# A convolution's last load in odd-sized pieces: 5, 120 and 3 partitions for the last quarter

## The chip, the cores and the metric

One core of a Trainium2 chip. The metric is the device time of one execution in microseconds (us). A ratio below is the mean time of one kernel's fast runs over that of the other's of the same rounds, so it is not quite the ratio of the medians that are quoted; an interval is a 95% interval. A few executions of 130.3 to 130.5 us are slow and count nowhere.

## The reference

```python
# x: (16, 64, 64, 64) float32, weight: (128, 64, 3, 3) float32, 90% zeros
x_pad = np.pad(x, ((0, 0), (0, 0), (1, 1), (1, 1)))
for b, co, ci, kh, kw in ...:      # five nested loops
    output[b, co] += weight[co, ci, kh, kw] * x_pad[b, ci, kh:kh+64, kw:kw+64]
# output: (16, 128, 64, 64) float32, 33.55 MB
```

## The kernel before

The 16 images go in 8 pairs; a pair fills 128 partitions (2 images of 64 channels). GpSimd issues the loads, which cast float32 to bf16 on the way (all but the weights and the first half of pair 0, which SyncE loads as they are); SyncE issues the stores. TensorE forms the products, GpSimd one sum of two rows per block, ScalarE and VectorE bring the results to the output tiles.

```python
xs = [x_pool.tile([128, H, W], BF16, name=f"x{p}") for p in range(NP)]   # all 8 pairs stay in SBUF
...
nc.gpsimd.dma_start(out=xs[0][:, HEAD:H, :], in_=pair(0)[:, HEAD:H, :])  # software queue
...
for p in range(1, NP):
    nc.gpsimd.dma_start(out=xs[p], in_=pair(p))       # 128 rows of 16 KB float32 -> 8 KB bf16
... # warm-up matmuls, weights
for p in range(NP):
    o = [o_pool.tile([C_OUT, H, W], FP32, name="o") for _ in range(2)]
    for blk in range(4):
        ... # GpSimd: s = even rows + odd rows of xs[p]; TensorE, ScalarE, VectorE: o
        if last and blk % 2 == 1:
            ... # store half of each o: 128 rows of 8 KB (4 stores in all)
    if not last:
        for n in range(2):
            nc.sync.dma_start(out=out[2 * p + n], in_=o[n])   # 128 rows of 16 KB (14 stores)
```

## Time and profile before

| | before |
|---|---|
| time, median | 127.65 us (3 runs), 127.64 (6 runs) |
| profiled execution | 127.12 us, span 125.4 us |
| last TensorE instruction | 110 us |
| last store issued / last landing | 111.8 / 124.2 us |
| bytes stored, share of the DMA engines' time | 66.2% of 16 engines' span, the loads 30.7% |

The page's rows of digits are tenths of busy time in 40 slices of the span. The lines that matter stand in the prediction. Beside them I used the trace's records of single DMA packets (queue, start, duration, size). A packet of an engine begins where the engine's last one ended, to a few ns, so in the last part of the run, with only stores left, the packets can be put together into 16 sequences, one for each DMA engine. Where loads and stores alternate this is ambiguous.

### The profile page before, as it was taken

The page shows a single profiled execution, that of the slowest core. Times are in us where ns is not written, and L with a number is a line of the kernel's source. Part 1 is how long each engine was busy: PE and PEld are TensorE (multiplying, and loading weights), DVE is VectorE, ACT ScalarE, POOL GpSimd, SP SyncE. Part 2 cuts the span into 40 slices and gives each one's busy share as a digit, 9 for nine tenths or more (in the row PEclk, how much of TensorE's full clock was granted, in tenths as well). Part 3 has the DMA queues.
Part 4 walks back from the last instruction along what each step waited for, and adds up shares of the span by engine and source line. Part 5 has one row for each costly group of instructions (what it writes and reads, how often), then busy time and mean ns, then how long its engine had stood idle before and what let it go on. Part 6 is the DMA issues. An engine that isn't in the chain of part 4 may idle for free.

```text
span 125.4 us, 2486 instructions
## 1 busy us (share of the span) xinstructions
PE 107.5 (86%) x1002; PEld 58.8 (47%) x1002; DVE 82.4 (66%) x135; ACT 39.0 (31%) x71; POOL 40.7 (32%) x45
## 2 busy tenths in 40 slices
PE   6679999999999999999999999999999999920000
PEld 6435555555555555555555555555555555500000
DVE  0463877877787778777877787778777877760000
ACT  4555323333333333333333333333333333300000
POOL 6936533333333333333333333333333300000000
PEclk9999999999999999999999999999999999997555
DMA  5999999989999999999999999999999999999980
GB/s 146 338 222 220 212 214 220 191 259 350 324 311 337 308 293 319 342 316 308 426 429 423 408 429 434 450 416 434 418 418 429 429 444 423 434 397 423 423 369 10
DMA packets 4044, 42.93 MB, mean 342 GB/s; under 512 B 448, under 2 KB 448, under 8 KB 704
## 3 DMA queue, kind: packets, MB, share of 16 engines
q1 hardware_dynamic: 2880, 34.90, 66.2%
q0 software_dynamic: 1152, 7.86, 30.7%
q8 instruction: 8, 0.13, 0.4%
q14 instruction: 4, 0.03, 0.1%
HBM read 17.07 MB, written 33.55 MB: 404 GB/s over the span
## 4 chain that ended last, share of the span: by engine, by line
PE 81%; DMA 4%; DVE 1%; issue 1%; DVEq 0%; SPq 0%
PE ps L135 81%; DMA o<-in_x_dram 4%; DVE o L168 1%; DVEq L214 0%; DVE x L87 0%; SPq L60 0%; DVEq L168 0%
## 5 line engine op out<-in xcount | busy, mean ns | idle before, releaser
L168 DVE TENSOR_TENSOR o<-ps,pc 128x512 f32<-128x512 f32 x124 | 77.8, 686 | 22.1 <-PE ps L135 19.8
L135 PE MATMUL ps<-x,wT 64*128 64x504 bf16 (+3 forms) x780 | 88.8, 373 | 1.5 <-DVE x L87 1.5
L135 PEld LDWEIGHTS <-wT 64*128 64x128 bf16 x966 | 55.2, 94 | 49.4 <-issue 1.5
L154 POOL TENSOR_TENSOR s<-x 128x512 bf16<-128x512 bf16 x31 | 35.6, 1152 | 57.7 <-PE ps L135 41.5
L161 ACT COPY pc<-ps 128x512 f32<-128x512 f32 x62 | 33.3, 589 | 64.0 <-issue 61.8
L135 PE MATMUL ps<-s,wT 64*128 64x512 bf16 (+1 forms) x186 | 25.7, 377 | 0.0
L74 PE MATMUL ps<-idle_rhs 128*128 128x128 bf16 x27 | 3.1, 310 | 1.0 <-DVE idle_rhs L71 1.0
L67 POOL DMA_DIRECT2D x<-in_x_dram x7 | 3.7, 561 | 0.0
L74 PEld LDWEIGHTS <-idle_rhs 128*128 128x128 bf16 x27 | 2.8, 144 | 1.0 <-DVE idle_rhs L71 1.0
L91 DVE CAST w_bf<-w_sb 128x192 bf16<-128x192 f32 (+1 forms) x4 | 1.3, 382 | 3.0 <-DMA w_sb<-in_weight_dram 3.0
L149 DVE COPY o<-ps 128x512 f32<-128x512 f32 x2 | 1.4, 692 | 2.0 <-PE ps L135 2.0
L148 ACT COPY o<-ps 128x512 f32<-128x512 f32 x2 | 1.2, 586 | 2.4 <-PE ps L135 2.4
L87 ACT CAST x<-o 128x576 bf16<-128x576 f32 (+1 forms) x2 | 1.5, 802 | 0.5 <-DMA o<-in_x_dram 0.5
L91 ACT ACT_TABLE_LOAD x1 | 1.3, 1283 | 0.7 <-PEq L203 0.7
L97 PE MATMUL ps<-ident,w_bf 128*128 128x128 bf16 x9 | 1.1, 292 | 0.4 <-DVE w_bf L91 0.4
L87 DVE CAST x<-o 128x576 bf16<-128x576 f32 x1 | 0.5, 460 | 1.4 <-DMA o<-in_x_dram 1.4
L91 ACT CAST w_bf<-w_sb 128x64 bf16<-128x64 f32 (+1 forms) x2 | 0.7, 418 | 1.9 <-DMA w_sb<-in_weight_dram 1.9
L97 PEld LDWEIGHTS <-w_bf 128*128 128x128 bf16 x9 | 0.8, 128 | 0.8 <-DVE w_bf L91 0.8
L101 DVE TENSOR_TENSOR wT<-ps,wT 128x384 bf16<-128x384 f32 x2 | 1.0, 550 | 0.0
L63 POOL DMA_DIRECT2D x<-in_x_dram x1 | 0.7, 696 | 0.8 <-POOLq L203 0.8
L71 DVE MEMSET idle_rhs<- 128x64 uint32 x1 | 0.1, 112 | 0.8 <-PEq L203 0.8
L110 ACT CAST wT<-ps 128x384 bf16<-128x384 f32 x1 | 0.5, 481 | 0.4 <-PE ps L97 0.4
(8 smaller groups left out, 1.9 us busy)
## 6 DMA issues: line engine op xcount, KB each, us to landing
out_dram<-o SPq DMA_DIRECT2D x14, 2048.0 KB, 19.8
x<-in_x_dram POOLq DMA_DIRECT2D x7, 1024.0 KB, 29.3
out_dram<-o SPq DMA_DIRECT2D x4, 1024.0 KB, 12.3
o<-in_x_dram SPq DMA_DIRECT2D x1, 1024.0 KB, 5.4
x<-in_x_dram POOLq DMA_DIRECT2D x1, 512.0 KB, 7.5
w_sb<-in_weight_dram SPq DMA_DIRECT2D x1, 288.0 KB, 3.1
```

The lines of the kernel that those rows point to most:

```text
L67: nc.gpsimd.dma_start(out=xs[p], in_=pair(p))
L74: nc.tensor.matmul(idle_ps, idle_rhs, idle_rhs, start=True, stop=True)
L87: copy(out=xs[0][:, a:b, :], in_=x_head[:, a:b, :])
L91: copy(out=w_bf4[:, g, a:b, :], in_=w_v[:, k : k + b - a, :])
L97: nc.tensor.matmul(wps[:, j, :], src, ident, start=True, stop=True)
L101: nc.vector.tensor_tensor(out=wT[:, g], in0=wps, in1=wT[:, G1], op=SUB)
L135: nc.tensor.matmul(ps[n][:, lo:hi, c_lo:c_hi], tap(g, kw, n), src[q, a:b:step, c_lo + kw - 1 : c_hi + kw - 1], start=(i == 0), stop=(i == ...
L148: nc.scalar.copy(out=o[0][:, r0 : r0 + rows, :], in_=ps[0])
L149: nc.vector.tensor_copy(out=o[1][:, r0 : r0 + rows, :], in_=ps[1])
L154: nc.gpsimd.tensor_tensor(out=s, in0=xs[p][:, r0 : r0 + 16 : 2, :], in1=xs[p][:, r0 + 1 : r0 + 16 : 2, :], op=ADD)
L161: nc.scalar.copy(out=c, in_=shared[n])
L168: nc.vector.tensor_tensor(out=o[n][:, first : r0 + 16 : 2, :], in0=ps[n], in1=pc[n], op=ADD)
```

## The change

Its intent: one DMA engine (number 4) ends last, so the last load is cut and issued such that GpSimd's rotation over the engines gives that engine the least.

```diff
-    for p in range(1, NP):
+    for p in range(1, NP - 1):
         nc.gpsimd.dma_start(out=xs[p], in_=pair(p))
...
+    PIECES = (            # (issued at pair, first and last partition, first and last image row)
+        (2, 0, 128, 0, 48),
+        (3, 0, 5, 48, 64),
+        (3, 5, 125, 48, 64),
+        (4, 125, 128, 48, 52),
+        (4, 125, 128, 52, 56),
+        (4, 125, 128, 56, 60),
+        (4, 125, 128, 60, 64),
+    )
     for p in range(NP):
...
+        for when, c0, c1, a, b in PIECES:
+            if when == p:
+                nc.gpsimd.dma_start(
+                    out=xs[NP - 1][c0:c1, a:b, :], in_=pair(NP - 1)[c0:c1, a:b, :]
+                )
```

## The prediction

> **What bounds the kernel now.** I read, in this order, the page's utilisation rows, the chain of waits, SyncE's own waits, a table of windows, and last the single DMA packet records of the trace (queue, start, duration, size of each; they do not name the DMA engine). The page first:
>
> ```profile
> PE   6679999999999999999999999999999999920000
> DVE  0463877877787778777877787778777877760000
> DMA  5999999989999999999999999999999999999980
> ...
> q1 hardware_dynamic: 2880, 34.90, 66.2%
> q0 software_dynamic: 1152, 7.86, 30.7%
> ```
>
> TensorE and VectorE stop about 15 us before the end. The DMA row is 9 from slice 2 to slice 38: the 16 DMA engines never rest, and the two queues' shares, 66.2% and 30.7%, fill the span. What ends the program is the last store, not arithmetic:
>
> ```profile
> SPq L188 <- DVE o L168: 92.2, 14, 19.9
> SPq L214 <- DMA out_dram<-o: 11.6, 4, 4.4
> ```
>
> The second line is SyncE waiting 11.6 us for the last stores after it issued them. The windows table (span, then busy times; last three columns are granted clock, DMA share, GB/s) shows how that end looks:
>
> ```profile
> 64.00:110.00 46.00, 46.00 (x434) 24.58 (x431) 35.89 (x58) 15.17 (x29) 12.97 (x12) 1.00 1.00 427
> ...
> 121.50:122.50 1.00, 0.00 (x0) 0.00 (x0) 0.00 (x0) 0.00 (x0) 0.00 (x0) 0.50 0.43 180
> 122.50:123.70 1.20, 0.00 (x0) 0.00 (x0) 0.00 (x0) 0.00 (x0) 0.00 (x0) 0.50 0.06 27
> ```
>
> A DMA share of 1.00 through 46 us, and 0.06 in the last 1.2 us. One engine of sixteen is 0.0625, so **a single DMA engine works alone at the end**. The 16 completion events of each store say the same. Those of the last store land at 121.3, 121.3, 121.4, 121.6, 121.8, 122.2, 122.4, 122.5, four at 122.6, 122.7, 122.8, 122.8 and **124.2** us. The kernel is bound by the most loaded DMA engine, which is 1.4 us behind the second. The mean is 122.3, so perfect balance would be worth 124.2 - 122.3 = 1.9 us (1.5%).
>
> Why that engine is late is in the packets. From 62.5 us on, when only stores are left, one unbroken sequence of 16 KB store packets takes 634 to 662 ns each, where 1295 of the 1792 take 611 ns. It fills 62.5 to 110.2 us, some 74 rows at 646 ns against a period of 608 ns (from a store to the next the first engine takes 4.86 us for 8 rows): 74 x 38 ns = 2.8 us, and this engine ends 2.9 us after the first. The 8 instruction fetches (16 KB, 882 to 967 ns each) seem to fall on other engines, since the two packets after a fetch that take about 1 us are not in the slow sequence; they would account for the eight or so engines 1.1 to 1.5 us behind the first. That the slow engine is number 4 I take from the change; nothing in this trace numbers it.
>
> **What the Trainium skill says.** "DMA: Bandwidth & Descriptors", section "Why a DMA increments its semaphore by 16 and not by 1": a DMA is spread over the largest k up to 16 that divides its outer size; a software DMA with k below 16 takes k consecutive engines from a round-robin cursor, and all 16 engines post its completion increment. So 128 partitions use 16 engines, 5 use 5, 120 use 15, and 3 use 3. The trace agrees for 128 (1152 = 8 x (128 rows + 16 increments)) and has no other size. The same section names an exception: some software copies use ceil(partitions/16) per engine without the cursor; then the aim would miss. Section "Queues, rings and completion order": each engine takes turns between its queues, packet by packet. The trace agrees: between 22 and 62 us loads and stores alternate. Section "Latency and other measured facts" says engines 7 and 15 are usually slower in traces; here one is slow, and its cause is not shown.
>
> **The change, part by part.** The bytes loaded and stored are unchanged. Removed: one whole load of the last pair (128 rows of 16 KB float32, written as 8 KB bf16). Added: rows 0 to 47 of the image for 128 partitions (12 KB read per partition), then the last quarter (4 KB per partition) as 5 + 120 + 3 partitions, the 3 cut again into four of 1 KB.
>
> *Cursor.* If it stands at engine 0 (the 128-partition loads leave it), the 5 go to engines 0 to 4, the 120 to engines 5 to 15 and 0 to 3, so all but engine 4, eight each, and the four of 3 to engines 4 to 15, one each. Engine 4 gets one quarter row and one 1 KB piece; engines 0 to 3 nine quarter rows; the others eight and a 1 KB piece.
>
> *Cost of one packet.* A load packet of 16 KB read takes 624 ns and one of 8 KB 322 ns (the half load of pair 0). A line through both gives 20 ns + 37.75 ns per KB: 12 KB = 473, 4 KB = 171, 1 KB = 58 ns (estimates). Completion increments take 9 or 22 ns; six more DMAs put six more on each engine, about 0.09 us.
>
> *Sum per engine*, for the last pair's load:
> - before, every engine: 8 x 621 (start to start) = 4.97 us
> - after, engine 4: 8 x 473 + 171 + 58 + 90 = 4.10 us, **-0.87**
> - after, engines 0 to 3: 8 x 473 + 9 x 171 + 90 = 5.41 us, **+0.44**
> - after, engines 5 to 15: 8 x (473 + 171) + 58 + 90 = 5.30 us, **+0.33**
>
> All engines are busy without a break, so each engine's end moves by its sum: the slow one from 124.2 to 123.3, the second from 122.8 to between 123.1 and 123.25. They meet near 123.3: gain **0.9 us**, all on the path that sets the end.
>
> *GpSimd.* One load issue of 0.56 us leaves the start, seven come in later: one after the sum at 21.57 us (so near 22.7), two after that at 34.37 (35.5), four after that at 47.18 (48.3 to 50.5). GpSimd waits about 2.0 us before nearly every sum and is 2 blocks of 3.2 us ahead of TensorE, so even 4 x 0.56 = 2.2 us is absorbed. Two of the small pieces wait on a semaphore shared with earlier loads (pairs 4 and 5, landed at 33.4 and 43.2 us): past by then. No TensorE, VectorE or ScalarE instruction is added or removed; the order of some products in the last pair moves a little. Worth: 0.
>
> *Loads must not run dry.* The sixth pair's load lands at 53.0 us, and the pieces are in the ring by 50.5, so the two queues go on alternating. The load's last quarter now alternates 4 KB pieces with 16 KB stores and ends later than the 62.8 us of before: 53 + 8 x (0.47 + 0.61) + 8 x (0.17 + 0.61) is about 68 us. The last pair's first sum is at about 88.8 us and its rows 48 to 63 are wanted after 98: 20 us or more of slack.
>
> **Rivals.**
> - *The rotation misses the slow engine* (the cursor starts elsewhere, or the exception holds). Then it takes +0.33 to +0.44 like any other: 124.6, or 128.0 us on the clock. For it: nothing in the trace numbers engines or shows a cursor. Against: 5, 120, 4 x 3 fit the cursor rule so exactly that the slow engine was probably seen by number. I give it 15%.
> - *The second engine becomes the bound earlier*: if small packets cost more than the line says (a fixed 60 ns rather than 20 adds 8 x 40 = 0.3 us to all), the others end at 123.5: 127.0 us. For it: eight or nine engines lie within 0.4 us below the second. Against: the 4-byte increments cost only 9 to 22 ns.
> - *The late issue leaves the load queue empty or delays GpSimd.* The store queue would fill the engines anyway (a store takes 10.6 to 29.3 us to land, so stores are backed up), and total work decides: 0 to +0.3 us. The instants above speak against it.
> - *The slow engine's lag exists only under the profiler.* The profiled run took 127.12 us against 127.65 us unprofiled, so the profiler costs nothing visible; but if the lag were smaller unprofiled, the gain would shrink towards 0.2 us: 127.4 us.
>
> **How the range follows.** 127.65 - 0.87 = 126.8 us, a ratio of 0.993. The best case is bounded by the second engine: at most 1.4 us gained if the pieces cost the others nothing, 126.3. The upper end takes in a lag that is smaller unprofiled and dear small packets, and just part of the miss: 127.8. Faster by 2% would need 2.55 us, more than the 1.9 us of perfect balance: 0.01. Slower by 2% would need +2.55 us, for which no term is at hand beyond an unforeseen stall: 0.02.
>
> **What the changed profile would show.** Right: the software queue has 7 x 144 + 144 + 21 + 136 + 4 x 19 = 1385 packets; the last store's latest completion comes at about 123.3 us, within 0.3 us of the second; DMA share stays at 1.00 from 64 to 110 us; one sequence of 640 to 660 ns store packets is still there; TensorE still stops near 110 us; the last pair's load lands near 68 us. Wrong: one engine still alone for over 1 us at the end (rotation missed, or the slow engine changed); several engines ending together past 123.5 us (pieces dearer than the line); a DMA share below 1 in the middle, or GpSimd waits named for DMA (late issue). An instruction fetch that moves onto the slow engine would cost 0.6 us or more and also break it.

## The result, and the profile after

The changed kernel takes **127.69 us** (median of 6 runs, 127.57 to 130.51, one of them slow) against 127.64 us; ratio 1.0003 (0.9989 to 1.0017). A second measurement, in other rounds (experiment 9), gave 1.0006 (0.9991 to 1.0020). The change moves nothing. I had forecast 126.8 us.

The page after, the same rows as the prediction shows of before:

```profile
PE   6669999999999999999999999999999999990000
DVE  0352278787778777877787778777877787774000
DMA  4999999999999999999999999999999999999990
...
q1 hardware_dynamic: 2880, 34.90, 66.1%
q0 software_dynamic: 1456, 7.87, 31.0%
```

The DMA engines are as full as before. The software queue has 1456 packets where I had counted 1385: 71 too many. The windows table after:

```profile
64.00:110.00 46.00, 46.00 (x434) 23.35 (x432) 36.27 (x58) 15.04 (x28) 13.86 (x13) 1.00 1.00 426
...
121.50:122.50 1.00, 0.00 (x0) 0.00 (x0) 0.00 (x0) 0.00 (x0) 0.00 (x0) 0.50 0.76 320
122.50:123.70 1.20, 0.00 (x0) 0.00 (x0) 0.00 (x0) 0.00 (x0) 0.00 (x0) 0.50 0.15 61
```

The DMA share in the last 1.2 us is 0.15, some 2.4 engines, where before it was 0.06, one engine. It looks as if the load had been levelled, and yet the last landing is later, 124.6 us against 124.2, with the second at 124.2. The span is 125.8 us against 125.4.

One difference between the two traces has nothing to do with the change. The timeline of TensorE, before and then after (start, duration, instructions):

```profile
7.12 3.99 PE L135 MATMUL ps<-x,wT 64*128 64x512 bf16 x36 [1.54 <-DVE x L87]
```

```profile
7.47 6.50 PE L135 MATMUL ps<-x,wT 64*128 64x512 bf16 x36 [2.03 <-DVE x L87]
```

The same 36 matmuls of the first pair took 3.99 us in one execution and 6.50 us in the other, and everything on TensorE after them is 2.87 us later, to the last. The Trainium skill, "TensorE: Matmul & The Clock Gate", section "What's actually happening", says that the start at half clock varies from run to run. This agrees: the kernel before, run again, had 6.72 us there (experiment 0). The granted clock stands in the trace too. In the first trace of before it is full from 5.3 us on, in experiment 0 and in the first trace of the changed kernel only from 13.0 and 12.6 us (the windows show 1.00 before the first clock record, so they hide this). In the other late traces it is full at first and goes back to half for 3.4 us, as in experiment 3 (first line before, second line experiment 3; the clock is the third number from the end):

```profile
9.00:10.00 1.00, 1.00 (x12) 0.56 (x10) 0.69 (x1) 0.59 (x1) 1.00 (x2) 1.00 1.02 213
9.00:10.00 1.00, 1.00 (x8) 0.40 (x6) 0.00 (x0) 0.00 (x0) 1.00 (x2) 0.50 0.86 180
```

So the trace that I predicted from was an execution with an **early start**, 127.12 us, and those with a late start are the usual ones (9 of the 13 traces).

### The profile page after: what moved, and what is told of

It is laid out like the page before. It is cut to its first block, busy times and chain, and to the rows that moved or that the text cites. A ratio compares the mean times of both kernels' runs of the same rounds, so it can differ in the third digit from the quotient of the medians.

```text
span 125.8 us, 2496 instructions
## 1 busy us (share of the span) xinstructions
PE 110.1 (88%) x1002; PEld 56.8 (45%) x1002; DVE 82.3 (65%) x135; ACT 39.0 (31%) x71; POOL 43.8 (35%) x51
## 3 DMA queue, kind: packets, MB, share of 16 engines
q1 hardware_dynamic: 2880, 34.90, 66.1%
q0 software_dynamic: 1456, 7.87, 31.0%
## 4 chain that ended last, share of the span: by engine, by line
PE 83%; DMA 5%; DVE 1%; issue 1%; DVEq 0%; SPq 0%
PE ps L135 83%; DMA o<-in_x_dram 5%; DVE o L168 1%; DVEq L232 0%; DVE x L87 0%; SPq L60 0%; DVEq L168 0%
## 5 line engine op out<-in xcount | busy, mean ns | idle before, releaser
L135 PE MATMUL ps<-x,wT 64*128 64x504 bf16 (+3 forms) x780 | 91.1, 381 | 2.0 <-DVE x L87 2.0
L135 PEld LDWEIGHTS <-wT 64*128 64x128 bf16 x966 | 53.2, 96 | 54.4 <-issue 5.0
L190 POOL DMA_DIRECT2D x<-in_x_dram x7 | 3.7, 527 | 0.0
L67 POOL DMA_DIRECT2D x<-in_x_dram x6 | 3.2, 559 | 0.0
L63 POOL DMA_DIRECT2D x<-in_x_dram x1 | 0.7, 710 | 0.8 <-POOLq L221 0.8
```

The source lines that it names most:

```text
L135: nc.tensor.matmul(ps[n][:, lo:hi, c_lo:c_hi], tap(g, kw, n), src[q, a:b:step, c_lo + kw - 1 : c_hi + kw - 1], start=(i == 0), stop=(i == ...
L190: nc.gpsimd.dma_start(out=xs[NP - 1][c0:c1, a:b, :], in_=pair(NP - 1)[c0:c1, a:b, :])
```

## The experiments

All outputs are right. "Slow stores" below are the 16 KB store packets of 630 to 670 ns; the usual duration is 611 ns. Each count takes in one or two before 48 us that are not part of the long sequence. In experiment 0 and in the first profile of the changed kernel packets of other engines, between 102 and 110 us, fall into that range too (102 and 91 in all), so those two counts are not used.

### 0. The kernel before again

> The kernel before, unedited, to learn how its trace varies. Theory A (in the changed kernel the slow DMA engine kept its full share, so the change moved nothing on the path): times 127.5 to 127.7 us, ratio 1.000, and again one DMA engine 1.2 to 1.6 us behind the second at the end. If the slow engine's lag is an accident of one execution (rival), the last store's 16 landings will end together here.

127.73 us, ratio 0.9982 (0.9938 to 1.0027). Its windows:

```profile
121.50:122.50 1.00, 0.00 (x0) 0.00 (x0) 0.00 (x0) 0.00 (x0) 0.00 (x0) 0.50 0.74 311
122.50:123.70 1.20, 0.00 (x0) 0.00 (x0) 0.00 (x0) 0.00 (x0) 0.00 (x0) 0.50 0.15 61
```

They are those of the changed kernel. The "levelling" above is no effect of the change. The last two landings are at 124.3 and 124.7 us. I had expected 1.2 to 1.6 us between them; it was 0.4. The sequences of packets show who the second is: the engine on which an instruction fetch (a packet of the queue that the page calls instruction) of 16 KB falls at 113.7 us, in the middle of its short stores. In the first trace of before the last fetch came at 110.1 us and fell on an engine that had time to spare. So the 1.4 us by which I let the slow engine be relieved was that of a lucky trace.

### 1 and 2. Marks that number the engines

In the kernel before, and in the changed one (with the first block too), tiny loads of a size each of its own:

```diff
+    for i, (parts, n, dt) in enumerate(      # experiment 2 only
+        ((1, 31, BF16), (1, 37, BF16), (1, 41, FP32), (1, 43, FP32), (3, 47, FP32), (120, 53, FP32))
+    ):
+        m = mark_pool.tile([128, n], dt, name=f"g{i}")
+        nc.gpsimd.dma_start(out=m[0:parts, :], in_=pair(0)[0:parts, 1, 0:n])
+    for k in range(1, 16):
+        m = mark_pool.tile([16, k + 16], FP32, name=f"m{k}")
+        nc.sync.dma_start(out=m[0:k, :], in_=pair(0)[0:k, 0, 0 : k + 16])
```

> The kernel before, with 15 tiny loads of 1, 2, ... 15 partitions issued by SyncE behind the last store, each of its own size. If such a load uses the lowest-numbered DMA engines, engine e gets 15-e of them right after its last store packet, so the order in which engines end can be numbered. Theory: the last engine to end carries 11 marks (number 4). If it carries another count, the change aimed at the wrong engine. About 1 to 2 us longer than before.

> The changed kernel with the same marks at the end, and six tiny GpSimd loads after its last sum: two of 1 partition with a cast, two of 1 partition without, one of 3 and one of 120 partitions without. Theory A (GpSimd gives ceil(partitions/16) partitions per engine from engine 0 on, with no cursor): all four single ones fall on one engine, the 3 on that and its two neighbours, the 120 leave out one engine; the engine with the light share of the last pair is number 15 (no mark after its last store), and the last to end is again number 4 with 9 quarter rows. Rival B (a cursor that rotates): the four single ones fall on four engines, and the light engine is another.

The times, 132.65 and 132.23 us, are those of the marks. SyncE's marks arrived too late to stand behind every engine's last store, but the first six did. The packet records name no engine: the numbers here are the order in which these marks take the engines up, the one with the mark of 1 partition being engine 0. In the kernel before, the sequence that ended at 121.22 us goes on with the marks of 1 to 5 partitions (engine 0), 121.71 with those from 2 on, 122.13 from 3, 122.63 from 4, 122.88 from 6 (engine 5), and **the last, 124.99 us, from 5 on: it is engine 4**. The change aimed at the right engine. Its 13 slow stores in the part I put together are the only such run.

In the changed kernel the last to end is engine 4 again, at 124.68 us. GpSimd's marks show the rule by which loads are spread. The packet records of these marks (start in us, bytes):

```
106.547  62 B    107.186  74 B    108.427  164 B    109.659  172 B     (the four of 1 partition)
110.118 188 B    110.605 188 B    110.891  188 B                       (the one of 3 partitions)
1696 B x 15                                                            (the one of 120 partitions)
```

The four single ones lie in one sequence, each one or two stores after the one before; the third of the 188 B follows on the fourth (109.659 + 1.232). That sequence ends at 122.02 us and carries mark 1: **engine 0, four times out of four, with a cast and without**. The other two 188 B marks lie on the sequences that carry marks 2 and 3: engines 1 and 2. The 120 partitions are 15 packets (8 rows each, joined); the one sequence without such a packet is the one that ends first, 121.53 us, and engine 4 has one.

So there is no cursor in these loads. A load of n partitions gives n/16, rounded up, of them to each engine from engine 0 on, and engines left over get placeholders of 4 bytes in the same number. Those are the 71 unforeseen packets exactly: 11 engines without one of the 5 partitions, 8 on the one engine without any of the 120, and 4 x 13 for the pieces of 3: 11 + 8 + 52 = 71. The same count fits the placeholders of experiments 5, 6 and 8 (48, 64 and 48), which came later. The engine spared is then the last, number 15, and engine 4 is one of the five that get a ninth quarter row. (That engine 4 had nine follows from the rule and from the two sequences that can be followed there; while loads and stores alternate, the sequences are not certain.)

### 3. The whole load, issued late

```diff
     PIECES = (
+        (2, 0, 128, 0, 64),
     )          # the other seven pieces are gone; the same form in all that follow
```

> One part of the change alone: the last pair's load whole, but issued at the second pair as the change does. Theory and rival alike: late issue is worth nothing, ratio 0.998 to 1.002; engine 4 (the one with the 634 to 662 ns stores) ends last by about 0.3 us, as in the rerun of before. If late issue itself cost or gained something that hid the change's gain, the ratio is 0.993 or 1.007.

127.62 us, ratio 0.9991 (0.9971 to 1.0010): late issue is worth nothing, as predicted. Engine 4 ends at 124.47 us with the second at 123.07 (last packets): 1.4 us here, where the rerun of before had 0.3 us.

### 4 and 10. Four column quarters for all engines alike

```diff
     PIECES = (
+        (2, 0, 128, 0, 16), (2, 0, 128, 16, 32), (3, 0, 128, 32, 48), (3, 0, 128, 48, 64),
     )
```

> The last pair's load in four column quarters of all 128 partitions, so every engine has 24 load packets more and none is favoured. Theory: engine 4's stores are slow only where a store follows a store; each load packet in between hides about 38 ns of it, so its slow sequence starts about 15 us later, some 24 slow stores fewer, and engine 4 gains 0.7 us on the others while all lose 0.1 to 0.2 us to the extra packets; its end falls to or below that of the engine with the last instruction fetch. Ratio 0.996 to 1.001. Rival (engine 4 is slow at all its stores, hidden or not): the number of slow stores does not fall and engine 4 still ends last, 0.2 us later than in the rerun: ratio 1.001 to 1.003.

> The four column quarters once more, on this chip, to see whether 0.9963 repeats: theory 0.995 to 0.998, with some 50 to 60 slow stores and engine 4 within 0.5 us of the second engine. Rival (the first result was chance): 0.999 to 1.001.

**127.16 us, ratio 0.9963 (0.9937 to 0.9989), and again 127.19 us, 0.9961 (0.9941 to 0.9982).** Every engine has more work here, and the kernel is faster. Slow stores: 54 and 56, against 81 with the whole load; the slow sequence begins at 77.0 and 74.8 us instead of 60.6. (The first of the two had an early start; the early trace of before has 76 slow stores, from 62.5 us on.) Engine 4 ends 0.3 to 0.5 us after the second engine. The windows of the whole load (experiment 3) and then of the second run of the quarters:

```profile
122.50:123.70 1.20, 0.00 (x0) 0.00 (x0) 0.00 (x0) 0.00 (x0) 0.00 (x0) 0.50 0.13 55
123.70:124.50 0.80, 0.00 (x0) 0.00 (x0) 0.00 (x0) 0.00 (x0) 0.00 (x0) 0.50 0.05 20
```

```profile
122.50:123.70 1.20, 0.00 (x0) 0.00 (x0) 0.00 (x0) 0.00 (x0) 0.00 (x0) 0.50 0.23 96
123.70:124.50 0.80, 0.00 (x0) 0.00 (x0) 0.00 (x0) 0.00 (x0) 0.00 (x0) 0.50 0.00 0
```

With the whole load an engine still works after 123.70 us (DMA share 0.05, the most of one engine); with the quarters more engines work up to that time (0.23 against 0.13) and hardly any after. So engine 4 is slow only where a store follows on a store; a load packet in between hides it. The rival (slow at every store) would have left the number as it was. Nor does it wait for the loads of all engines to end: in experiment 8 its slow sequence begins at 71.2 us, while load packets of other engines go on to 75.2. The profiles agree start for start: 126.80 us against 127.12 of before with an early start, 127.26 against 127.74 with a late one. Nor is the gain a mix of early and late starts: sorted by the granted clock that each run lists (0.955 and below, 0.956 to 0.962, 0.970 and above), the runs with quarters have means of 127.22, 127.05 and 127.34 us, those of before in the same rounds 127.72, 127.59 and 127.64.

### 5, 6 and 8. Work really taken from engine 4

By the rule of experiment 2 a load of 4 partitions lands on engines 0 to 3, which have room. No set of partitions under this rule gives engine 4 less than engine 5: what an engine gets never rises with its number. So all of 4 to 15 are relieved together.

```diff
     PIECES = (       # experiment 5
+        (2, 0, 112, 0, 64), (3, 112, 128, 0, 32),
+        (4, 112, 116, 32, 64), (4, 116, 120, 32, 64), (4, 120, 124, 32, 64), (4, 124, 128, 32, 64),
     )
     PIECES = (       # experiment 6
+        (2, 0, 112, 0, 64), (3, 112, 128, 0, 16), (3, 112, 116, 16, 64), (4, 116, 120, 16, 64),
+        (4, 120, 123, 16, 64), (4, 123, 126, 16, 64), (4, 126, 128, 16, 64),
     )
     PIECES = (       # experiment 8
+        (2, 0, 112, 0, 20), (2, 0, 112, 20, 42), (3, 0, 112, 42, 64), (3, 112, 128, 0, 32),
+        (4, 112, 116, 32, 64), (4, 116, 120, 32, 64), (4, 120, 124, 32, 64), (5, 124, 128, 32, 64),
     )
```

> Work really taken from engine 4 by the rule that the marks showed (a GpSimd load of 4 partitions lands on engines 0 to 3): the last pair's load as 112 partitions, 16 partitions for rows 0 to 31, and rows 32 to 63 of those 16 as four loads of 4 partitions. Engines 4 to 15 lose half a row (0.31 us), engines 0 to 3, which end 1.3 us or more before engine 4, gain one and a half (0.93 us). Theory: end 0.4 to 0.6 us earlier, ratio 0.995 to 0.997. Rival (the end of the program is not set by the last DMA engine): ratio 1.000.

> The same with a larger dose: rows 16 to 63 of the 16 partitions as loads of 4, 4, 3, 3 and 2 partitions. Engines 4 to 15 lose three quarters of a row (0.47 us), engines 0 to 3 gain 4.25, 4.25, 3.25 and 1.25 times 12 KB less that: about 1.9, 1.9, 1.4 and 0.5 us. Theory: end 0.6 to 0.8 us earlier, ratio 0.994 to 0.996, with engines 0 and 1 now close to the last. Rival: 1.000.

> Candidate for a version better than both: the last pair's load as three column pieces of 112 partitions (hiding 16 more slow stores), and of the other 16 partitions rows 32 to 63 as four loads of 4 partitions, which land on engines 0 to 3. Theory: engine 4 loses 0.3 us of load and 0.5 us of slowness, the other late engines 0.2 us: ratio 0.994 to 0.997. Rival (the hiding alone counts and less load on engines 4 to 15 brings nothing, as the small effect of the first such run could be read): 0.997 to 0.998.

| experiment | median | ratio (interval) | end of engine 4, of the second (last packets) |
|---|---|---|---|
| 5, half a row | 127.50 us | 0.9988 (0.9971 to 1.0004) | 124.38, 123.43 |
| 6, three quarters of a row | 127.44 us | 0.9979 (0.9959 to 0.9998) | 123.56, 123.28 |
| 8, half a row, and three column pieces | 127.31 us | 0.9975 (0.9959 to 0.9990) | 123.54, 123.47 |

The direction is as expected, the sizes are about half of it or less; experiment 5 alone is not clear of zero. In experiment 5 engine 4 lost half a row (0.31 us by my line) and ended 0.09 us earlier than in experiment 3. The effect of experiment 4 in reverse does not explain it: engine 4 still has eight load packets (seven whole rows and a half one), and the slow stores are 77 against 81. Two late traces of a whole load differ by 0.2 us themselves (124.27 in experiment 0, 124.47 in experiment 3), so one trace of each cannot size it; it stays open. Experiments 6 and 8 had the early start in their profile, so their ends are to be set against the first trace of before (123.74 and 122.48): engine 4 ends 0.2 us earlier. Experiment 8 was meant to beat the quarters and does not; its ratio lies in the range of its rival (0.997 to 0.998, the hiding alone counts), so this run does not show a gain from the relief of engine 4.

### 7. The change without its odd pieces

```diff
     PIECES = (
+        (2, 0, 128, 0, 48), (3, 0, 128, 48, 64),
     )
```

> The change without its odd pieces: the last pair's load as rows 0 to 47 and rows 48 to 63, each of all 128 partitions. It keeps the split that hides 8 more of engine 4's slow stores and leaves out the 5, 120 and 3 partitions. Theory: engine 4 gains about 0.3 us by the split against 0.05 us for the extra packets, ratio 0.998 to 0.999, the number of slow stores about 8 below the whole load's (81 on the early start of the first pair, up to 102 on the late one). Rival (the odd pieces cost nothing and the split brings nothing): 1.000.

127.79 us, ratio 1.0017 (0.9998 to 1.0035). The slow stores fell as expected (72 against 81, beginning at 66.1 us), and in the profile engine 4 ends at 124.20 us, 0.27 us before that of experiment 3. The time did not follow: a miss. One run of 128.3 us weighs in it, and the interval reaches 1.000; what the split alone is worth in time stays open within some 0.3%.

### 9. The changed kernel again

> The changed kernel once more, beside the others on one chip: ratio 0.998 to 1.001; one engine ends first by some 0.5 us or is among the first, engine 4 ends last with 9 to 12 slow stores fewer than the whole load has, and no engine is alone for more than 1.5 us.

127.72 us, ratio 1.0006 (0.9991 to 1.0020), 71 slow stores (some three of them of other engines), the sequence from 66.7 us on, one engine first at 121.14 us, engine 4 last at 124.23, the second at 123.30.

## Why the prediction was wrong

- **What bounds the kernel: held.** The DMA share is 1.00 from 64 to 110 us before and after (the row of digits before has an 8 in slice 9, where I read 9 throughout), and in every profile that I put together the engine with the slow stores is the last to end. That it is engine 4 the marks show.
- **The step that failed: "Cursor. If it stands at engine 0 ..., the 120 to engines 5 to 15 and 0 to 3, so all but engine 4".** There is no cursor for these loads. Experiment 2 put the same engine under all four single loads and the same three under the 3; the 71 placeholders agree to the packet. The engine spared is number 15 by this rule, one that has no part in the end. This was my first rival, at 15%, and the exception that the Trainium skill's page names; I should have given it more than the rule, since the page says of the exception, and not of the cursor, that it was measured.
- **The rival's size was wrong too.** I gave a miss 128.0 us: +0.33 to +0.44 us on the slow engine. It cost nothing (ratio 1.0003 and 1.0006). "Each engine's end moves by its sum" left out that engine 4's stores are slow only back to back. More load packets mean more stores with one between: its slow sequence begins at 64.6, 65.6 and 66.7 us in the three traces with the change's pieces, against 59.6, 60.6 and 61.7 in the three of a whole load with a late start. 5.0 us less, at 38 ns per store of 646 ns, are 0.3 us, about what the ninth quarter row and the extra packets add. Experiment 4 shows the effect by itself; this sum for the changed kernel is worked out, not measured apart, and experiment 7 did not confirm it in time. The ends do not contradict it: with a late start engine 4's last packet is at 124.16 and 124.23 us in the changed kernel, at 124.27 and 124.47 with a whole load (experiments 0 and 3).
- **The prize was taken from one trace.** "1.4 us behind the second" was 0.3 in the rerun, 1.4 in experiment 3, 0.9 in the second trace of the change (last packets). The second is often the engine that an instruction fetch happens to hit near the end. With a gap of 0.3 us even the right rotation would have gained nothing by the prediction's own sums, since the second engine was to end 0.33 us or more later (an estimate). It cannot be tried: no pieces under this rule spare engine 4 alone.
- **Packet costs: held.** 12, 4 and 1 KB packets took 473, 172 and 59 ns (473, 171 and 58 by the line). From start to start the split costs 15 ns a row (a 12 KB load and a store 1074, a 4 KB load and a store 773, a 16 KB load and a store 1225, a store alone 607: 467 + 166 against 618), not 23.
- **Late issue, GpSimd, dry queue: held.** Experiment 3 is 0.9991; the DMA share never dips.
- **The lag exists only under the profiler: not tested.** The record does not say which executions, if any, ran without the profiler: each run lists a span and a granted clock.

## What to carry to other kernels

When every DMA engine is full to the end, look at the engines one by one; but take the gap between the last and the second from several executions, because one engine's lead can be an accident of where an instruction fetch fell. Before you aim a load at particular engines, mark them: a few tiny loads of distinct sizes show in one run where GpSimd and SyncE put their shares. And if one engine is slow at stores that follow each other, try more and smaller load packets for all, spread over the stores, before moving work away: four column quarters gave 0.996 of the time before, the best version here, where moving work away gave 0.998 to 0.999 (the intervals overlap).

## What the Trainium skill lacked or had wrong

- "DMA: Bandwidth & Descriptors", section "Why a DMA increments its semaphore by 16 and not by 1": a round-robin cursor for software loads with fewer than 16 engines was not seen here. Loads of 1 partition (with a cast and without) fell on engine 0 four times of four, one of 3 on engines 0 to 2, and 120 partitions on 15 engines at 8 each. The "exception" was the rule in all six marks.
- The same page does not have the placeholders: an engine without a share gets as many 4-byte packets as the others get rows; 71 of them in the changed kernel, 9 or 22 ns each.
- The same page, section "Latency and other measured facts", names engines 7 and 15 as the slower ones. Here it is engine 4: 16 KB stores of the hardware queue of 633 to 668 ns against 611, only where a store follows a store, and the last of them at 109.9 to 113.4 us, within 0.9 us of TensorE's end in every trace, though a few 16 KB stores of 611 to 629 ns follow on that engine. The cause stays open.
- "Runtime: NRT & Kernel Launch", section "Instruction fetch mechanics", has fetches of 16 KiB blocks, which agrees (8 packets of 16384 bytes), and calls their cost mostly hidden. Here each holds one DMA engine for 878 to 996 ns, and one at 113.7 us put that engine second to last, at 123.95 us.
- No page that I read says how much the end of a DMA-bound kernel varies with the start of TensorE: the traces whose first pair ran early (first store issued at 21.6 to 21.7 us) took 126.8 to 127.1 us, those with a late start (23.5 to 24.7) 127.3 to 127.9, over several kernels. The clock records go with it: full from 5.2 to 5.6 us on in the early ones, for good only from 10.7 to 13.0 us in the late ones. No run set the start, so the size of its effect on one kernel was not measured apart.
